# A row-streaming matmul on one core: stores moved from their own DMA ring to the ring of the loads, in a fixed order

## The chip, the core and the metric

The kernel runs on one core of a Trainium2 chip. The metric is device time in microseconds (us) of one execution, as the median of several runs. A separate profiled execution gives the trace.

## What is computed

The reference adapts a weight matrix with a low-rank product, scales each column to a given magnitude, and multiplies a long matrix of rows with it (a DoRA forward pass):

```python
batch, seq_len, in_dim, out_dim, rank = 16, 2048, 256, 256, 16
W_adapted = W + scale * (lora_A @ lora_B)
W_norm = np.sqrt(np.sum(W_adapted ** 2, axis=0, keepdims=True) + 1e-8)
W_final = W_adapted / W_norm * m
y = x.reshape(-1, in_dim) @ W_final          # (32768, 256) @ (256, 256), float32
```

The weights are small. The rows x and the result y are 33.55 MB each, and each crosses between the chip's memory (HBM) and the core's on-chip memory (SBUF) once.

## The kernel before

The 32768 rows are cut into 8 blocks (NBLK) of 4096 rows. A block is one SBUF tile `x_sb` of 128 partitions x 32 rows x 256 floats, 4 MiB. Each partition holds 32 consecutive rows, so that a transfer of a block consists of 128 pieces of 32 KB. There are five such tiles (XBUFS = 5), used in turn. The result of a block is written over the rows in the same tile, and stored from there.

At the start, small transfers bring the weights, and SP issues the loads of blocks 0 to 4 (L62, called from L77 and L78). Meanwhile the final weights `w_final` are computed (L94 to L132), once.

The main loop (L184) goes over 64 chunks (NCH), 8 (CH) per block. `transposed` casts a chunk of the rows to bf16 on GpSimd (POOL, L148), transposes it on TensorE (PE, L151), and copies the transposed chunk from PSUM to SBUF on VectorE (DVE, L155). `multiplied` does the matmuls (L166), and ScalarE (ACT, L174) copies the product over the rows in `x_sb`. In general the transposition of the next chunk is issued ahead of the product of the present one. At the last chunk of a block the product goes first.

After the last chunk of block b, ACT issues the block's store (L176). Then SP issues the load of block b+5 into the same tile (L181, which calls L62); it waits until that store has landed. The instruction order on each engine is the order of the program text. A DMA issued from SP goes to SP's ring, queue q1 in the profile; one issued from ACT to ACT's ring, queue q10. Both rings are served by the same 16 DMA engines. A transfer has landed when all of them have finished their parts.

Of the kernel before, what the change touches and what calls it, by code (L numbers as in the profile page):

```python
# [11 lines left out]
def kernel(  # L12
# [10 lines left out]
    nc = tc.nc  # L23
# [15 lines left out]
    NBLK = N // BLK  # L39
# [3 lines left out]
    XBUFS = 5  # L43
# [16 lines left out]
    def load_x(b):  # L60
        t = xpool.tile([P, DJ, IN], FP32, name="x_sb", tag="x_sb")
        nc.sync.dma_start(  # L62
            out=t,
            in_=x_flat[b * BLK : (b + 1) * BLK].rearrange("(p j) k -> p j k", p=P),
        )
        x_tiles[b] = t
# [93 lines left out]
    def multiplied(g):  # L160
        b, c = divmod(g, CH)
        xt = xts.pop(g)
        y_ps = pp_y.tile([P, J, OUT], FP32, tag="psy", name="y_ps")
        for t in range(KC):
            for j in j_order:
                nc.tensor.matmul(  # L166
                    y_ps[:, j, :],
                    xt[:, j * P : (j + 1) * P, t],
                    w_final[:, t, :],
                    start=(t == 0 and (j % (J // 2)) == 0),  # L170
                    stop=(t == KC - 1 and (j % (J // 2)) == (J // 2) - 1),
                )

        nc.scalar.copy(out=x_tiles[b][:, c * J : (c + 1) * J, :], in_=y_ps)  # L174
        if c == CH - 1:
            nc.scalar.dma_start(  # L176
                out=out_flat[b * BLK : (b + 1) * BLK].rearrange("(p j) k -> p j k", p=P),
                in_=x_tiles[b],
            )
            if b + XBUFS < NBLK:  # L180
                load_x(b + XBUFS)  # L181

    transposed(0)
    for g in range(NCH):  # L184


        first = (g + 1) % CH == 0
        if first:
            multiplied(g)
        if g + 1 < NCH:  # L190
            transposed(g + 1)
        if not first:
            multiplied(g)
# [35 lines left out]
```

## Time and profile before

| what | value |
|---|---|
| median of 5 runs | 165.04 us |
| lowest and highest of them | 164.5 and 170.71 us |
| the profiled execution's own time | 168.44 us |
| its span, first to last instruction | 166.6 us |
| mean granted TensorE clock in it | 0.873 |
| TensorE / ScalarE / GpSimd / VectorE busy | 62% / 40% / 40% / 30% |
| bytes moved by DMA, mean rate | 67.53 MB, 405 GB/s |
| from issue to landing, median of the 8 loads and of the 8 stores | 39.4 and 34.8 us |

The profiled execution is 3.4 us longer than the median of the runs: its durations are summed against 168.44 us. The page divides the span into 40 equal slices; a digit is the busy share in tenths. In DMA rows, the time from issue to landing includes the time that a transfer stands behind others on the rings. Times in the views count from the first instruction. The stores were issued at 30.81, 41.90, 52.99, 69.38, 90.07, 110.28, 130.99 and 151.46 us.

### The profile page before, as it was taken

The page shows a single profiled execution, that of the slowest core. Times are in us where ns is not written, and L with a number is a line of the kernel's source. Part 1 is how long each engine was busy: PE and PEld are TensorE (multiplying, and loading weights), DVE is VectorE, ACT ScalarE, POOL GpSimd, SP SyncE. Part 2 cuts the span into 40 slices and gives each one's busy share as a digit, 9 for nine tenths or more (in the row PEclk, how much of TensorE's full clock was granted, in tenths as well). Part 3 has the DMA queues.
Part 4 walks back from the last instruction along what each step waited for, and adds up shares of the span by engine and source line. Part 5 has one row for each costly group of instructions (what it writes and reads, how often), then busy time and mean ns, then how long its engine had stood idle before and what let it go on. Part 6 is the DMA issues. An engine that isn't in the chain of part 4 may idle for free.

```text
span 166.6 us, 2032 instructions
## 1 busy us (share of the span) xinstructions
PE 103.0 (62%) x778; PEld 86.0 (52%) x778; DVE 50.7 (30%) x76; ACT 66.4 (40%) x67; POOL 66.3 (40%) x70
## 2 busy tenths in 40 slices
PE   1174799999994699306993089920899109990000
PEld 0043588898893499204992069810698107980000
DVE  0219444444541335103350034400344003440000
ACT  3010257678576057500575007740077400773000
POOL 1007667685820972009720197101970019700000
PEclk9999999999999789975999759996599965999655
DMA  5999999999999899999999999999999999997980
GB/s 201 484 393 464 417 441 441 374 378 441 441 397 472 386 474 397 405 449 401 393 464 397 456 401 433 433 417 378 449 413 456 409 472 393 417 452 338 393 378 16
DMA packets 2635, 67.53 MB, mean 405 GB/s; under 512 B 433, under 2 KB 450, under 8 KB 578
## 3 DMA queue, kind: packets, MB, share of 16 engines
q1 hardware_dynamic: 1296, 33.82, 48.6%
q10 hardware_dynamic: 1330, 33.59, 47.1%
q8 instruction: 6, 0.10, 0.2%
q14 instruction: 3, 0.02, 0.0%
HBM read 33.85 MB, written 33.55 MB: 405 GB/s over the span
## 4 chain that ended last, share of the span: by engine, by line
DMA 53%; PE 28%; DVE 5%; ACT 2%; issue 1%; POOL 1%; ACTq 0%; POOLq 0%; SPq 0%
DMA out_dram<-x_sb 25%; DMA x_sb<-in_x_dram 25%; PE y_ps L166 18%; PE xt_ps L151 8%; DMA b_nat<-in_lora_B_dram 3%; ACT x_sb L174 2%; PE n_ps L118 1%; DVE xt L155 1%; DVE w_final L132 1%; DVE rnorm L130 1%; PE mb_ps L123 1%; POOL xb L148 1%; DVE wam L128 0%; DVE sq L113 0%; DVE wa L109 0%
## 5 line engine op out<-in xcount | busy, mean ns | idle before, releaser
L148 POOL CAST xb<-x_sb 128x1024 bf16<-128x1024 f32 x64 | 65.6, 1048 | 78.8 <-DMA x_sb<-in_x_dram 64.8
L174 ACT COPY x_sb<-y_ps 128x1024 f32<-128x1024 f32 x64 | 64.4, 1013 | 75.2 <-POOL xb L148 38.8
L166 PE MATMUL y_ps<-w_final,xt 128*128 128x256 bf16 x512 | 71.7, 289 | 1.6 <-DVE xt L155 1.6
L155 DVE COPY xt<-xt_ps 128x512 f32<-128x512 f32 x64 | 44.0, 691 | 88.1 <-PE xt_ps L151 88.1
L151 PE MATMUL xt_ps<-identity,xb 128*128 128x128 f32 x256 | 44.2, 306 | 37.7 <-POOL xb L148 37.7
L166 PEld LDWEIGHTS <-xt 128*128 128x128 bf16 x512 | 51.5, 103 | 12.0 <-DVE xt L155 4.8
L151 PEld LDWEIGHTS xt_ps<-identity,xb 128*128 128x128 f32 x256 | 34.1, 159 | 42.3 <-POOL xb L148 41.4
L120 ACT ACTIVATE norm<-n_ps,eps_col 128x256 f32<-128x256 f32 x1 | 0.5, 474 | 7.6 <-PE n_ps L118 7.6
L118 PE MATMUL n_ps<-sq,ones 128*128 128x256 f32 x4 | 2.0, 667 | 1.6 <-DVE sq L113 1.6
L98 PE MATMUL aT_ps<-identity,a_nat 128*16 128x128 f32 x2 | 0.6, 394 | 3.7 <-DMA a_nat<-in_lora_A_dram 3.7
L118 PEld LDWEIGHTS n_ps<-sq,ones 128*128 128x128 f32 x4 | 1.2, 324 | 2.2 <-issue 2.0
L104 PE MATMUL ab_ps<-b_bf,aT 16*128 16x256 bf16 x2 | 0.6, 402 | 2.8 <-DVE aT L100 2.8
L88 ACT ACT_TABLE_LOAD x1 | 1.3, 1283 | 2.2 <-issue 2.2
L98 PEld LDWEIGHTS aT_ps<-identity,a_nat 128*16 128x16 f32 x2 | 0.1, 90 | 3.7 <-issue 3.7
L94 DVE CAST b_bf<-b_nat 16x256 bf16<-16x256 f32 x1 | 0.3, 281 | 5.4 <-DMA b_nat<-in_lora_B_dram 5.4
L104 PEld LDWEIGHTS <-aT 16*128 16x128 bf16 x2 | 0.1, 104 | 3.2 <-DVE aT L100 3.2
L132 DVE TENSOR_TENSOR w_final<-wam,rnorm 128x256 bf16<-128x256 f32 x2 | 1.8, 921 | 0.0
L130 DVE RECIPROCAL rnorm<-norm 128x256 f32<-128x256 f32 x1 | 1.7, 1745 | 0.0
L125 DVE COPY m_all<-mb_ps 128x256 f32<-128x256 f32 x1 | 0.4, 425 | 3.4 <-PE mb_ps L123 3.4
L123 PE MATMUL mb_ps<-m_row,ones 1*128 1x256 f32 x2 | 1.2, 710 | 0.0
L109 DVE SCALAR_TENSOR_TENSOR wa<-ab_ps,w_nat 128x512 f32<-128x512 f32 x1 | 0.7, 691 | 0.7 <-PE ab_ps L104 0.7
L123 PEld LDWEIGHTS mb_ps<-m_row,ones 1*128 1x128 f32 x2 | 0.5, 308 | 0.7 <-issue 0.7
(12 smaller groups left out, 3.2 us busy)
## 6 DMA issues: line engine op xcount, KB each, us to landing
x_sb<-in_x_dram SPq DMA_DIRECT2D x8, 4096.0 KB, 39.4
out_dram<-x_sb ACTq DMA_DIRECT2D x8, 4096.0 KB, 34.8
w_nat<-in_W_dram SPq DMA_DIRECT2D x1, 256.0 KB, 2.7
a_nat<-in_lora_A_dram ACTq DMA_DIRECT2D x1, 16.0 KB, 2.9
b_nat<-in_lora_B_dram ACTq DMA_DIRECT2D x1, 16.0 KB, 5.2
m_row<-in_m_dram ACTq DMA_DIRECT2D x1, 1.0 KB
```

Of the source, the lines that this page charges most:

```text
L88: nc.scalar.activation(out=warm, in_=eps_col, func=AF.Sqrt)
L98: nc.tensor.transpose(aT_ps[:, t * P : (t + 1) * P], a_nat[:, t, :], identity)
L104: nc.tensor.matmul(ab_ps[:, t, :], aT[:, t * P : (t + 1) * P], b_bf, start=True, stop=True)
L118: nc.tensor.matmul(n2_ps, ones, sq[:, t, :], start=(t == 0), stop=(t == KC - 1))
L123: nc.tensor.matmul(mb_ps, ones[0:1, :], m_row, start=True, stop=True)
L130: nc.vector.reciprocal(out=rnorm, in_=norm)
L132: nc.vector.tensor_mul(out=w_final[:, t], in0=wam[:, t], in1=rnorm)
L148: nc.gpsimd.tensor_copy(out=xb, in_=rows)
L151: nc.tensor.transpose(xt_ps[:, j * P : (j + 1) * P], xb[:, j, :].bitcast(FP32), identity)
L155: nc.vector.tensor_copy(out=xt.rearrange("p r t -> p (r t)").bitcast(FP32), in_=xt_ps)
L166: nc.tensor.matmul(y_ps[:, j, :], xt[:, j * P : (j + 1) * P, t], w_final[:, t, :], start=(t == 0 and (j % (J // 2)) == 0), stop=(t == KC - ...
L174: nc.scalar.copy(out=x_tiles[b][:, c * J : (c + 1) * J, :], in_=y_ps)
```

## The change

All stores are issued by SP instead of ACT, so that loads and stores stand on one ring. The load that refills a tile is issued one block later: after store b, SP issues the load of block b+4, into the tile whose result was stored by store b-1. On SP the order becomes: loads 0 to 4, store 0, store 1, load 5, store 2, load 6, store 3, load 7, stores 4 to 7. A load still waits for the landing of the store that frees its tile, and a store for the last copy of its block.

```diff
         nc.scalar.copy(out=x_tiles[b][:, c * J : (c + 1) * J, :], in_=y_ps)
         if c == CH - 1:
-            nc.scalar.dma_start(
+            nc.sync.dma_start(
                 out=out_flat[b * BLK : (b + 1) * BLK].rearrange("(p j) k -> p j k", p=P),
                 in_=x_tiles[b],
             )
-            if b + XBUFS < NBLK:
-                load_x(b + XBUFS)
+            if b >= 1 and b - 1 + XBUFS < NBLK:
+                load_x(b - 1 + XBUFS)
```

## Prediction

> **What bounds the kernel now.** I read the busy table first, then the row of DMA shares in the 40 slices, the queue table, the chain of waits, and last the stretches of time and single transfers.
>
> ```profile
> span 166.6 us, 2032 instructions
> ...
> PE 103.0 (62%) x778; PEld 86.0 (52%) x778; DVE 50.7 (30%) x76; ACT 66.4 (40%) x67; POOL 66.3 (40%) x70
> ...
> DMA  5999999999999899999999999999999999997980
> q1 hardware_dynamic: 1296, 33.82, 48.6%
> q10 hardware_dynamic: 1330, 33.59, 47.1%
> q8 instruction: 6, 0.10, 0.2%
> ...
> x_sb<-in_x_dram SPq DMA_DIRECT2D x8, 4096.0 KB, 39.4
> out_dram<-x_sb ACTq DMA_DIRECT2D x8, 4096.0 KB, 34.8
> ```
>
> No compute engine is busy for more than 62% of the span, while the 16 DMA engines stand at nine tenths from the second slice to nearly the last. Queue q1 carries SP's ring (loads), q10 ACT's ring (stores), 33.8 and 33.6 MB. The third queue, 6 packets of instructions, will matter. In the chain, the two transfers stand for half of the span, and the long DMA pieces follow on each other:
>
> ```profile
> 52.99 42.36 DMA out_dram<-x_sb
> 95.41 41.05 DMA x_sb<-in_x_dram
> 136.60 1.05 POOL xb L148
> ```
>
> So a store issued at 52.99 takes 42 us, because it shares the engines with loads, and the load behind it another 41. A latency, however, is no loss while the engines are full. Whether they are full is in the stretches (columns: us, five engines' busy time, TensorE's clock, DMA share, GB/s):
>
> ```profile
> 3.00:30.00 27.00, 18.65 (x111) 13.89 (x112) 11.96 (x18) 8.45 (x11) 11.61 (x11) 1.00 1.00 430
> 30.00:36.00 6.00, 5.65 (x53) 5.07 (x51) 3.37 (x5) 3.85 (x5) 4.97 (x5) 1.00 0.98 358
> 36.00:53.00 17.00, 15.51 (x139) 13.58 (x137) 7.52 (x11) 13.04 (x13) 8.46 (x9) 1.00 1.01 433
> 53.00:135.00 82.00, 50.52 (x384) 42.76 (x384) 22.14 (x32) 32.20 (x32) 32.46 (x32) 0.85 1.00 424
> ...
> 150.00:154.00 4.00, 0.33 (x4) 0.05 (x1) 0.00 (x0) 1.43 (x2) 0.00 (x0) 1.00 0.81 344
> ```
>
> Loads alone on one ring run at 430 GB/s, and loads and stores alternating on two rings at 433. That is one rate, so 4 MiB cost 4.19 MB / 430 = 9.75 us, and I measure losses against it. When the first store joins (30 to 36) the rate is 358: 6 x (1 - 358/430) = 1.0 us lost. From 53 to 135, 82 x (1 - 424/430) = 1.1 us. From 150 to 154, 4 x (1 - 344/430) = 0.8 us, while the last store waits for its block. A packet is booked where it starts, so a window's edge can be off by one 32 KB packet on each of 16 engines, 0.52 MB: the 1.1 has an error of 1.2, and even the 1.0 is only good to a factor of two.
>
> The last two stores, each asked for alone:
>
> ```profile
> out_dram<-x_sb ACTq DMA_DIRECT2D x1, 4096.0 KB, 24.8
> ...
> out_dram<-x_sb ACTq DMA_DIRECT2D x1, 4096.0 KB, 14.0
> ...
> 130.99 0.34 ACTq L176 DMA_DIRECT2D out_dram<-x_sb  x1
> 151.46 0.34 ACTq L176 DMA_DIRECT2D out_dram<-x_sb  x1
> ```
>
> Store 6 lands at 131.0 + 24.8 = 155.8 and store 7 at 151.5 + 14.0 = 165.5, that is 9.7 us later: a full-rate transfer and nothing between. A landing is counted when the slowest of the 16 engines is through. So the engine that ends last had no pause before store 7. The 0.8 us at 150 to 154 were lost on engines that are ahead of it, and are worth nothing at the end. Why is one behind? The average engine needs 67.5 MB / 430 = 157 us and starts at about 3, so it could end at 160. If the 0.10 MB of instruction packets run on one engine, whose share of the rate is 430/16 = 26.9 GB/s, that one is 3.7 us later: 163.7. Add the losses of 1.0 and 1.1 and it ends at 165.8, where 165.5 is seen. That one engine fetches them all is my inference; the sum fits it.
>
> **The change, part by part.** It moves eight stores from ACT's ring to SP's, and lets the load of block b+4 follow store b (load 5 after store 1, 6 after 2, 7 after 3). No byte, packet, cast, matmul or copy is added or removed.
>
> *The issue.* ACT loses 8 issues of 0.34 us. They lie between copies of an engine that is 40% busy: worth 0. SP gets them; between its load issues it does nothing but wait.
>
> *The new order, by 9.75 us steps.* Load 0 lands at 1.2 + 12.5 = 13.7, loads 1 to 4 at 23.4, 33.2, 42.9, 52.7. Blocks are computed in about 11.1 us when loaded (stores issued at 30.8, 41.9, 53.0), so stores 0 and 1 stand on the ring when load 4 ends: 62.4 and 72.2. Load 5, issued at 62.4, lands at 81.9, then store 2 (91.7), load 6 (101.4), store 3 (111.2), load 7 (120.9), stores 4 to 7 (130.7, 140.4, 150.2, 159.9).
>
> *The added waits.* SP now waits for a block's last copy (L174) before each store, and for the store one block earlier before loads 5 to 7. Behind a waiting load stand the later stores. Load 5 waits for store 0 while store 1 still has 9.75 us on the ring; load 6 waits for store 1, 72.2, with load 5 and store 2 ahead of it, 19.5 us; load 7 for store 2, 91.7, with load 6 and store 3 ahead. What does a restart take? Before, store 0 landed at 30.8 + 24.7 = 55.5 and the load waiting for it was issued at 55.63, some 0.1 us later. The Trainium skill ("DMA: Bandwidth & Descriptors", the section on the anatomy of one DMA) gives a fixed 2.0 us per transfer, for its GpSimd path. By the row three waits would show 0.3 us, by the page about 6, if the ring were empty; since at least 9.75 us stand there, the sum takes 0 by either. The slowest engine's 3.7 us lag comes off that cover and leaves about 6.
>
> *Compute as a bound.* Block 7 lands at 120.9. In the trace, block 7's cast began at 136.60 and its store was issued at 151.46, 14.9 us. So store 7 is ready at 136 and is needed at 150: 14 us of room. Blocks 5 and 6 are ready at 97 and 116, needed at 131 and 140. TensorE's reduced clock (0.85) is in the 14.9.
>
> *Direction changes within the ring.* There are seven (load 4 to store 0, ..., load 7 to store 4), and before shows none inside one ring. From above: a cold start, load 0's 12.5 less 9.75, some 2.7 us, each: 19 us. From below: 0, or a gain, if switching once per 4 MiB is better than once per packet. The nearest row is 36 to 53, where every engine changes direction with every packet at 433 GB/s. I take 0.
>
> *What goes.* The 1.1 us from 53 to 135 and the 1.0 us at the first store lie where two rings are active and are lost on every engine, the slowest too. If the second ring causes them, 2.1 us go. From below 0: the first store's stall may belong to the first write and move to 52.7. Here a rule speaks against the change: the same page of the skill ("Issuing engines are not separate DMA queues") says that transfers issued by several engines run on the same 16 DMA engines and interleave, and that spreading them saves only issue time. By the rule the ring is indifferent and the gain is 0; by the rows it is up to 2.1. The 430 against 433 are on the rule's side, the 358 is not.
>
> **Sum.** The profiled execution took 168.44: a span of 166.6 and 1.84 around it. With all 2.1 gone the slowest engine ends at about 163.4, span 164.5, time 166.3. But the median of the runs shown is 165.04, 3.4 below that execution, and the lowest is 164.5. The ordinary runs must lack some of the profiled delays, and these stalls are the first candidates. I count two fifths of 2.1, 0.8 us, in ordinary runs: 165.04 - 0.8 = 164.2.
>
> **Rivals.**
> *No change* (about 165.0): the bytes bound, the ring makes no odds, and the slowest engine has the same packets as before. For it: 430 = 433, and 9.7 us between the last two landings. Against it: the 358.
> *All of it*: the stalls are in the ordinary runs too, 165.04 - 2.1 = 162.9. If the slowest engine also lags less there, so that the pause before store 7 reaches the end, another 0.8 goes: 162.1. Against it: the median's 3.4 us.
> *Slower, by direction changes in one ring*: if the engine finishes the last load's writes before it begins to read for the store, each change leaves a hole. At 0.4 us, 7 x 0.4 = 2.8, less the 1.1 that go with the two rings: 166.7. It decides from (1.1 + 0.5) / 7 = 0.23 us a change. For it: the stalls of before also come where transfers begin. Against it: alternation by the packet at the full rate, though there two rings supply the work.
> *The change doesn't do what it says*: if load 5 were ready only after store 1 is through, each of three loads would leave 2 us idle. The 9.75 us of cover speak against it.
>
> **How the numbers follow.** A measurement tells about 0.3%, 0.5 us, from no change. A small gain, 164.2 (163.7 to 164.7): 0.36. No change: 0.27. All of it: 0.15. Slower, including holes for unknown reasons: 0.22. Of the small gain about a fifth falls within 0.5 us and of no change a little falls on the faster side by scatter, so faster 0.46, same 0.31, slower 0.23. The range: 162.0 (all, with the pause) to 167.0 (direction changes at the price above), with more expensive ones left out.
>
> **What would show it.** Right: q10 nearly empty, q1 with 67 MB; x lands at about 43 and 53 for blocks 3 and 4 instead of 54.2 and 75.1; from 55 to 125 GB/s near 430 with no stretch of 358; SP's wait for stores moved under a full ring; the last store's issue near 136, with a landing over 25 us later. Wrong: rates under 420 between 53 and 125, holes at 52, 72, 82, 92, or the last landing at 165.5 or later in a comparable execution. If stretches are all at 430 and the time is still 165, the stalls were not in ordinary runs.

## The result and the profile after

The changed kernel takes 165.41 us (median of 44 runs, 164.86 to 166.14). Its ratio to the kernel before is 1.0017, with a 95% interval of 1.0004 to 1.003: slower by 0.17%. The interval lies above 1, but the difference is less than the 0.3% that the prediction gives as the least a measurement can tell from no change. The forecast had been 164.2, a gain of half a per cent. Left out of the ratio are long runs, more than 1.5% above a kernel's fastest, which only kernels with two rings had in number: 35 of 79 of the kernel before (median of all 79: 166.23 us, highest 173.08) and 12 of 22 of its variant below, against none of these 44 and 1 of 104 of the other one-ring runs; why is not known.

The profiled execution of the changed kernel took 165.36 us. These are its page's span, DMA shares and queues, and the landings of stores 6 and 7, counted in us from their issue:

```profile
span 163.5 us, 2035 instructions
...
DMA  5998999999999999999999999999999999999991
...
q1 hardware_dynamic: 2448, 67.37, 96.7%
q8 instruction: 6, 0.10, 0.2%
q10 hardware_dynamic: 178, 0.03, 0.1%
...
out_dram<-x_sb SPq DMA_DIRECT2D x1, 4096.0 KB, 33.3
...
out_dram<-x_sb SPq DMA_DIRECT2D x1, 4096.0 KB, 23.0
```

All large transfers are now in q1. The order on SP, from its timeline (start, us from the first to the last of the group, instruction, count):

```profile
1.16 2.90 SPq L62 DMA_DIRECT2D x_sb<-in_x_dram  x5
30.31 11.44 SPq L178 DMA_DIRECT2D out_dram<-x_sb  x2
65.50 0.34 SPq L62 DMA_DIRECT2D x_sb<-in_x_dram  x1
65.94 0.64 SPq L178 DMA_DIRECT2D out_dram<-x_sb  x1
75.18 0.34 SPq L62 DMA_DIRECT2D x_sb<-in_x_dram  x1
75.61 0.38 SPq L178 DMA_DIRECT2D out_dram<-x_sb  x1
94.55 0.34 SPq L62 DMA_DIRECT2D x_sb<-in_x_dram  x1
94.98 44.77 SPq L178 DMA_DIRECT2D out_dram<-x_sb  x4
```

Stores 6 and 7 were issued at 119.44 and 139.42, so they landed at 152.7 and 162.4: again 9.7 us apart, with nothing between. Load 5 landed at 65.50 + 19.3 = 84.8. Now the stretches of the prediction, and the one in which the first store begins (last column: GB/s):

```profile
3.00:30.00 27.00, 18.64 (x114) 13.94 (x114) 12.31 (x19) 8.94 (x11) 11.84 (x12) 1.00 1.00 429
30.00:36.00 6.00, 5.65 (x53) 5.20 (x53) 3.16 (x6) 3.85 (x5) 4.96 (x6) 1.00 1.01 429
48.00:56.00 8.00, 7.65 (x71) 6.72 (x69) 3.94 (x6) 5.85 (x6) 5.70 (x7) 1.00 1.03 389
56.00:135.00 79.00, 52.52 (x416) 45.18 (x414) 23.53 (x35) 34.42 (x36) 34.17 (x34) 0.83 1.00 431
135.00:159.00 24.00, 3.29 (x30) 2.58 (x27) 1.38 (x2) 3.80 (x4) 0.00 (x0) 0.61 1.01 433
```

The 358 of 30 to 36 us has become 429, but 389 has appeared at 48 to 56, where the ring goes from load 4 to store 0. After that the rate is 431 to the end. The stall has moved with the first store; it has not gone. In the packets of the trace it stands at the end of load 4: those that start from 50.5 to 51.1 take 1.65 to 2.03 us, and two of them 3.14 and 3.21, where 1.21 is usual.

Since a window counts whole packets at their start, I worked out the losses more finely: each packet's bytes are spread evenly over its duration, so that only what lies inside a window counts, and time lost is the window less bytes / 430 GB/s. (A steady stretch then comes out at 0 to -0.3, as its rate is 431 to 433.) In what follows "lost" means this, averaged over the 16 engines.

| execution | first large change of direction | later |
|---|---|---|
| before, the profile shown (168.44 us) | 0.90 us (30 to 38) | 1.26 us (53 to 135) |
| changed kernel (165.36 us) | 0.98 us (48 to 56) | -0.23 us (56 to 135) |

### The profile page after: what moved, and what is told of

Its sections match the earlier page's. It is cut to its first block, busy times and chain, and to the rows that moved or that the text cites. A ratio compares the mean times of both kernels' runs of the same rounds, so it can differ in the third digit from the quotient of the medians.

```text
span 163.5 us, 2035 instructions
## 1 busy us (share of the span) xinstructions
PE 99.4 (61%) x778; PEld 84.1 (51%) x778; DVE 50.5 (31%) x76; ACT 66.3 (41%) x67; POOL 66.5 (41%) x70
## 4 chain that ended last, share of the span: by engine, by line
DMA 60%; PE 16%; DVE 4%; ACT 2%; issue 1%; POOL 1%; ACTq 0%; SPq 0%; POOLq 0%
DMA out_dram<-x_sb 39%; DMA x_sb<-in_x_dram 18%; PE y_ps L166 9%; PE xt_ps L151 5%; DMA b_nat<-in_lora_B_dram 3%; ACT x_sb L174 2%; PE n_ps L118 1%; DVE w_final L132 1%; DVE rnorm L130 1%; PE mb_ps L123 1%; POOL xb L148 1%; DVE wam L128 0%; DVE wa L109 0%; DVE sq L113 0%; PE ab_ps L104 0%
## 5 line engine op out<-in xcount | busy, mean ns | idle before, releaser
L174 ACT COPY x_sb<-y_ps 128x1024 f32<-128x1024 f32 x64 | 64.3, 1012 | 63.2 <-PE y_ps L166 42.4
L166 PE MATMUL y_ps<-w_final,xt 128*128 128x256 bf16 x512 | 69.6, 283 | 2.3 <-DVE xt L155 2.3
L151 PE MATMUL xt_ps<-identity,xb 128*128 128x128 f32 x256 | 42.6, 299 | 28.5 <-POOL xb L148 28.5
L166 PEld LDWEIGHTS <-xt 128*128 128x128 bf16 x512 | 50.6, 101 | 12.2 <-DVE xt L155 5.8
L151 PEld LDWEIGHTS xt_ps<-identity,xb 128*128 128x128 f32 x256 | 33.0, 155 | 31.9 <-POOL xb L148 31.1
```

What stands on the lines that cost most here:

```text
L151: nc.tensor.transpose(xt_ps[:, j * P : (j + 1) * P], xb[:, j, :].bitcast(FP32), identity)
L166: nc.tensor.matmul(y_ps[:, j, :], xt[:, j * P : (j + 1) * P, t], w_final[:, t, :], start=(t == 0 and (j % (J // 2)) == 0), stop=(t == KC - ...
```

## The experiments

**The kernel before, profiled once more.** No edit.

> The kernel before, profiled once more, to see which of its stalls belong to an ordinary execution. Theory A (the 1.1 us between 53 and 135 us are a feature of two rings): the rate there is again near 424 GB/s against 430, and the first store's stretch (30 to 36 us) is again near 358. Theory B (the 1.1 us belong to a disturbed execution): with a span near 163.3 instead of 166.6, the rate from 53 to 135 is 428 or more, and only the first store's stall of about 1 us is left. Rival C (the span differs for another reason): span near 163.3 with both stalls as before.

It took 164.62 us, span 162.8, close to the fastest of the first five runs.

```profile
30.00:36.00 6.00, 5.65 (x53) 5.08 (x51) 2.95 (x5) 4.15 (x5) 4.29 (x5) 1.00 1.01 374
53.00:135.00 82.00, 54.00 (x398) 45.23 (x399) 23.53 (x34) 32.85 (x33) 36.36 (x37) 0.80 1.00 430
```

Theory B holds. From 53 to 135 us the two rings run at 430, not 424; the lost time there is -0.20 us. Only the first store's stall is left, 0.84 us (32 to 40). So the 1.1 us of the prediction was a property of the execution that the profile had caught, not of every execution with two rings.

**A small store at the start**, in both kernels, to see whether the first write as such is what costs.

```diff
+    touch = startup.tile([P, 32], FP32)
+    nc.vector.memset(touch, 0.0)
+    nc.scalar.dma_start(
+        out=out_flat[(NBLK - 1) * BLK : NBLK * BLK].rearrange("(p j) k -> p j k", p=P)[:, 0, 0:32],
+        in_=touch,
+    )
```

> The changed kernel with one small store (128 pieces of 128 bytes, into rows that the last store overwrites) issued from ACT at the start. Theory A (the stall at 48 to 53 us belongs to the core's first write to HBM): the stall is gone from 48 to 53, the rate there is near 430 instead of 406, all 16 engines land load 4 within about 1.5 us of each other, and the time is 1 to 3 us less than the changed kernel's 165.4. Theory B (the stall belongs to the first store on SP's ring, or to the change of direction under load): 406 again at 48 to 53, time 165.4 within 0.3. Rival C: the small store at the start holds up the weights and the first load, and the time is up to 1 us more.

165.17 us, ratio to the kernel before 1.0004 (0.9979 to 1.0028). Lost from 48 to 56: 0.91 us. The stall is there as before: theory B.

> The kernel before with the same small store from ACT at the start. Theory A (first write to HBM): the stretch from 30 to 36 us runs near 430 GB/s instead of 358 and the time falls by 1 to 3 us. Theory B (a stall of the first large store under load): 358 again, no change of time within 0.3%.

Ratio 1.0011 (0.9975 to 1.0048), and 380 GB/s from 30 to 36: the stall is there too, with 0.60 us lost from 30 to 38, somewhat smaller. Its profile has a span of 168.9 us, and from 53 to 135 it lost 1.03 us; the first profile of the kernel before (span 166.6) lost 1.26 there.

**One ring, but each load right behind its own block's store.** This undoes the second part of the change.

```diff
-            if b >= 1 and b - 1 + XBUFS < NBLK:
-                load_x(b - 1 + XBUFS)
+            if b + XBUFS < NBLK:
+                load_x(b + XBUFS)
```

> Stores on SP's ring, but each load follows its own block's store at once, as in the kernel before. SP waits for store b to land before load b+5 and before it may issue store b+1, so the ring runs empty between each store and its load, and load and next store stand behind. Theory (the later load is what keeps the single ring full): three holes of 2 to 2.7 us at load 5, 6 and 7, plus the spread of the 16 engines of about 3 us at each, so 6 to 15 us more than the kernel before, 171 to 180. Rival (the ring stays full through something else): within 0.5 us of 165.4.

178.74 us, ratio 1.0826 (1.0779 to 1.0873): as the theory said. The holes are plain (second and fourth row), and after them stands something I had not looked for (third and fifth row):

```profile
48.00:56.00 8.00, 7.65 (x70) 6.77 (x68) 3.70 (x6) 5.55 (x7) 5.92 (x6) 1.00 1.01 389
62.00:69.00 7.00, 6.65 (x61) 5.90 (x60) 3.20 (x6) 4.87 (x5) 4.98 (x6) 1.00 0.52 174
72.00:80.00 8.00, 2.24 (x20) 1.62 (x18) 0.69 (x1) 2.98 (x3) 0.37 (x1) 0.80 0.97 363
86.00:92.00 6.00, 6.00 (x57) 5.41 (x55) 3.43 (x5) 4.65 (x5) 2.08 (x2) 1.00 0.50 169
96.00:104.00 8.00, 0.36 (x2) 0.36 (x3) 0.00 (x0) 0.00 (x0) 1.45 (x2) 0.58 0.95 348
128.00:172.00 44.00, 12.51 (x96) 10.54 (x96) 5.53 (x8) 8.04 (x8) 7.05 (x7) 0.66 1.01 436
```

The first row is not a hole but the familiar stall at the first store. The holes, rows 2 and 4 and a third from 110 to 117, lost 4.2, 3.5 and 3.4 us. But where the load that follows a hole gives way to the next store (72 to 80, 96 to 104, and 120 to 128), 1.0, 1.1 and 1.1 us are lost, as at the first store. In the changed kernel the same changes from load to store cost nothing. What differs? After a hole all 16 engines start together. The landings in the trace show it: load 5's last part here comes 1.8 us after its first (77.7 to 79.5), most of them within 0.6, while in the changed kernel load 5 lands from 81.8 to 84.8. So the first store may be dear not because it is the first, but because the engines are still in step: all at the same point of their work.

**Store and load in turn from the start.** Loads 0 to 2, store 0, load 3, store 1, and so on.

```diff
-    for b in range(XBUFS):
+    for b in range(3):
         load_x(b)
...
-            if b >= 1 and b - 1 + XBUFS < NBLK:
-                load_x(b - 1 + XBUFS)
+            if b + 3 < NBLK:
+                load_x(b + 3)
```

> One ring as in the changed kernel, but store and load strictly in turn from the start: loads 0 to 2, store 0, load 3, store 1, load 4, and so on, load b+3 behind store b. Theory (the stall of about 1 us belongs to the first large store, wherever it stands, and costs the slowest engines 2 to 3 us): the stretch 48 to 53 us runs at 430 GB/s, the stall is at 30 to 36, and the time is 165.2 within 0.5. Rival (the stall of the changed kernel belongs to five loads queued ahead of the store, or to the ring's first refill): the stall stays near 48 to 53, or is gone, and the time falls by 1 to 3 us.

165.85 us, ratio 1.0054 (1.0023 to 1.0084). Neither expectation is right: at the first change (31 to 39) only 0.12 us are lost, but 0.99 at the second (39 to 47, store 0 to load 3) and 0.80 at the third (48 to 56, load 3 to store 1); afterwards nothing (-0.09 from 56 to 135).

```profile
31.00:39.00 8.00, 7.65 (x70) 6.90 (x69) 4.54 (x7) 5.51 (x6) 6.67 (x7) 1.00 1.08 457
39.00:47.00 8.00, 7.65 (x70) 6.76 (x69) 3.58 (x7) 5.59 (x6) 5.71 (x7) 1.00 0.99 375
48.00:56.00 8.00, 4.53 (x41) 3.73 (x39) 2.08 (x3) 4.74 (x5) 0.00 (x0) 1.00 0.97 373
```

The cost is not tied to the first store, nor to the direction from load to store. But the cheap first change speaks against the idea of engines in step: 15 of load 2's 16 parts had landed within 0.3 us (32.8 to 33.1). Store 0 had been issued at 31.47, only 1.3 us before its turn at about 32.8; why this change was cheap is not settled.

**Half of the matmuls.** Only the first 128 input columns are multiplied (`for t in range(1)` in the product, the stop flags to match); what is left out is the other half of the product.

> The changed kernel without the second half of the product (only the first 128 input columns are multiplied, 256 matmuls fewer), bytes unchanged. Theory A (compute is far from the bound, and instruction packets are a small part of the slowest engine's time): the instruction packets of 16 KB fall from 6 to 4 and the time from 165.4 by 0 to 0.7. Theory B (the prediction's: all instruction packets run on the one slowest engine, 0.6 us each): the time falls by 1.2 us. Rival C (compute does bound somewhere): the time falls by more than 2 us.

165.49 us, ratio 1.0018 (0.9992 to 1.0043), with four instruction packets of 16 KB instead of six:

```profile
q8 instruction: 4, 0.07, 0.2%
```

Two packets less should have freed the slowest engine of 1.2 us by the prediction's inference. Nothing came, which is theory A. TensorE is off the path, and not all instruction packets run on the engine that ends last. A second late engine does not hide a gain: the last three parts of store 7 land at 161.8, 162.5 and 162.6, in the changed kernel at 161.5, 162.3 and 162.4.

**Nine tiny loads behind the last store**, to see which engines end last.

```diff
+    for n, k in enumerate((15, 14, 12, 8, 7, 6, 4, 2, 1)):
+        probe = startup.tile([P, 32], FP32, name=f"probe{n}")
+        nc.sync.dma_start(out=probe[0:k, :], in_=x_flat[0:k, 0:32])
```

> The changed kernel with nine tiny loads (15, 14, 12, 8, 7, 6, 4, 2 and 1 partitions of 128 bytes) on SP's ring behind the last store. A load of k partitions lands in k parts, on k of the engines; each part stands behind the last store's packets on its engine, so the landings tell how far behind each group of engines is. Theory A: one and the same one or two engines are 3 us behind from the first store on, and they show in some of the groups and not in others. Theory B: the spread is shared over many engines: all groups show it alike. The time is that of the changed kernel plus 1 to 3 us.

One execution, 166.88 us. The parts of three of these loads landed at (us, from the trace's semaphore updates; each load is some 0.2 us later than the one before):

```
7 partitions: 160.2 160.9 160.9 161.1 162.8 163.4 163.5
6 partitions: 160.4 161.0 161.1 161.3 163.0 163.6
4 partitions: 160.6 161.2 161.3 161.5
```

The Trainium skill ("DMA: Bandwidth & Descriptors", the section on why a DMA increments its semaphore by 16) says that such a transfer of k partitions runs on the k lowest-numbered engines. The lists are nested as that wants. Going from 7 to 6 loses the latest part, from 6 to 4 the two that were then latest: counted from 0, engine 6, and engines 4 and 5, are the late ones, 1.7 us or more behind the other four. It is theory A with three engines. In the changed kernel the spread is there before 56 us: load 3's parts land from 42.4 to 42.8, but for one at 44.2; load 4's from 52.6 to 53.2, but for two at 55.7; store 7's from 159.2 to 162.4. So one engine is late before the stall, two are 2.5 us late after it, and 3.1 of the final spread of 3.2 us are there when it ends. (The landings carry no engine numbers, so that these are the same engines is likely, not shown.)

**Engines out of step from the start.** To test the idea of engines in step: extra loads on few engines, ahead of the others, of rows that are loaded again afterwards. These loads alone add bytes. (`load_x` then takes the tiles made here; that part of the edit is not shown.)

```diff
+    for b in range(XBUFS):
+        first_tiles[b] = xpool.tile([P, DJ, IN], FP32, name="x_sb", tag="x_sb")
+    for b, k in ((2, 12), (3, 8), (4, 4)):
+        nc.sync.dma_start(out=first_tiles[b][0:k], in_=x_flat[b * BLK : (b + 1) * BLK].rearrange("(p j) k -> p j k", p=P)[0:k])
     for b in range(XBUFS):
         load_x(b)
```

> The changed kernel with three extra loads at the start, of 12, 8 and 4 partitions of 32 KB (rows that are loaded again afterwards). They run on the first 12, 8 and 4 DMA engines, so that the engines reach the first store in four groups, 1.2 us apart, instead of together. 24 extra packets of 1.21 us on 16 engines are 1.8 us on the average and 3.6 us on the first four. Theory A (the stall comes from all engines changing from loads to stores at the same moment): the loss of 1.0 us on the average, 406 GB/s at 48 to 53, is spread out or gone; from 48 to 62 us the mean rate is 425 or more, and the time is 0.5 to 2 us above the changed kernel's, not 3. Theory B (the stall belongs to the first large store as such): the loss stays at about 1 us on each group, and the time is 2 to 4 us above.

176.98 us, ratio 1.0722 (1.0681 to 1.0763): the time misses both expectations, for a reason of its own. The extra loads and those behind them ran at 136 GB/s from 3 to 18 us. But from there on the kernel is at full rate, and the stall is gone: the first store now begins as load 4's parts land, from 63.3 to 67.1.

```profile
58.00:74.00 16.00, 15.65 (x143) 14.19 (x142) 7.92 (x12) 11.85 (x12) 12.12 (x13) 1.00 1.00 425
74.00:135.00 61.00, 38.07 (x300) 32.25 (x298) 16.80 (x25) 26.36 (x27) 22.12 (x22) 0.84 1.00 432
```

Lost from 58 to 74: 0.09 us.

**The same without extra bytes**: the load of block 1 in parts of 112, 12 and 4 partitions.

```diff
+        rows = x_flat[b * BLK : (b + 1) * BLK].rearrange("(p j) k -> p j k", p=P)
+        for lo, hi in ((0, 112), (112, 124), (124, 128)) if b == 1 else ((0, P),):
+            nc.sync.dma_start(out=t[lo:hi], in_=rows[lo:hi])
```

> The changed kernel with the load of block 1 in three parts of 112, 12 and 4 partitions, on 16, 12 and 4 engines: engines 0 to 3 carry one packet more (1.21 us), engines 12 to 15 one less. The last landings of the tiny loads put engines 4 to 6 last, 2.5 to 3 us behind the first, and 0 to 3 in the first half. Theory A (moving together is what stalls): the stall is smaller for the slowest engines and the time falls by 0.5 to 1.5 us, below both kernels. Theory B (the first store as such): the slowest engines carry what they carried, time as the changed kernel's within 0.3 us.

178.32 us, ratio 1.0809 (1.0769 to 1.0848): neither theory's time. It was to be the version that beats both kernels, and the split load spoiled it:

```profile
12.00:39.00 27.00, 14.86 (x98) 11.68 (x96) 10.47 (x14) 8.05 (x8) 8.47 (x8) 0.90 0.99 195
58.00:74.00 16.00, 15.65 (x143) 14.19 (x142) 7.87 (x13) 11.75 (x13) 12.12 (x12) 1.00 1.01 430
```

27 us at under half of the rate lost 14 us. Again the engines arrive out of step (load 4's parts land from 65.2 to 68.4), and the first store, which follows, costs next to nothing: 0.05 us lost from 58 to 74.

**Out of step, with every fourth partition.** The same extra loads, but of partitions 0, 4, 8 and so on, so that each of the few engines serves its own group of partitions.

```diff
-    for b, k in ((2, 12), (3, 8), (4, 4)):
+    for b, k in ((4, 4), (3, 4)):      # the other kernel: ((4, 8),)
-        ...[0:k]
+        ...[0 : 4 * k : 4]
```

> The changed kernel with two extra loads at the start, each of the 4 partitions 0, 4, 8, 12 (32 KB each, loaded again afterwards): two packets more, 2.4 us, on the first four DMA engines alone, which had 2.2 us or more to spare at the end. Theory A (the stall is 16 engines changing direction together, and every fourth partition keeps one engine to one group of partitions): the loads run at 430 GB/s from 8 us on; engines 0 to 3 reach the first store 2.4 us behind the others; the stall from 48 to 56 us falls from 1.0 to 0.7 or less; time within 1 us of 165.4. It beats both kernels only if the three last engines are spared. Theory B (the stall is that of a first store, the skew only hid it): still 1.0, and time 165.4 to 167.

> As before, but one extra load of the 8 partitions 0, 4, ..., 28: one packet more, 1.2 us, on the first eight engines. Two groups of eight, 1.2 us apart, instead of sixteen together. Theory A: the stall from 48 to 58 us is half of 1.0 or less, and the time is that of the changed kernel plus 1.2 us (three of the last engines are among the eight) less what they are spared of the stall, 164.5 to 166. Theory B: the stall stays at 1.0, time 166.5 or more.

The loads now run near full rate from 8 to 30 us: at 427 GB/s with eight engines delayed, and with four:

```profile
8.00:30.00 22.00, 13.36 (x86) 10.52 (x85) 8.45 (x13) 5.66 (x7) 10.07 (x10) 1.00 1.00 430
```

For the stall, whole packets are too coarse (405 to 408 GB/s from 48 to 62 in both and in the changed kernel). By bytes within the window:

| kernel | intended at the first store | parts of load 3 land | lost from 48 to 62 us |
|---|---|---|---|
| changed kernel | all together | over 1.8 us (15 within 0.4) | 1.05 us |
| one packet more on 8 engines | two groups of 8 | over 2.2 us | 0.61 us |
| two packets more on 4 engines | 4 behind 12 | over 2.7 us (11 within 0.4) | 0.36 us |
| load 1 in parts (58 to 74 us) | not in groups | over 3.2 us | 0.05 us |
| 12, 8 and 4 partitions (58 to 74 us) | four groups | over 3.8 us | 0.09 us |

From 1.05 us down to under 0.1, the loss is smaller where the engines are further apart. That is in favour of theory A, and the first store as such is excluded. But it is a trend in five kernels, each with other side effects, and two changes in the alternating kernel do not fit: the cheap first one, and the fourth (store 1 to load 4), which cost nothing (-0.02 us from 59 to 67) although 13 of load 3's 16 parts had landed within 0.4 us and all within 2.3. So spread is not the whole condition.

The expectations are met only in part. With four engines delayed the stall is in the range, but the time is 166.49 (ratio 1.0102, 1.0078 to 1.0126), 1.1 above the changed kernel instead of within 1; with eight, 0.61 us is more than the half expected, and the time of 167.14 (1.0105, 1.004 to 1.0169) is theory B's. The slow start of the extra loads, 321 and 357 GB/s from 3 to 8 us, costs more than the stall gives back. No version here beats the two kernels.

## Why the prediction was wrong

*What it had right.* The bound: with half of the matmuls the time stayed where it was. The order on the ring and its cover: from 56 us on the ring is never empty, and one_ring_old_order shows what happens without the later load, 13 us more. The waits of SP cost nothing. Compute has room: store 7 was issued at 139.4 for a turn at about 150 (forecast: 136). The pause before store 7 was worth nothing: the second profile of the kernel before has none (store 7 was issued at 145.82, store 6 landed at 152.0), and 9.7 us between the last two landings stayed. Changes of direction inside the ring were put at 0: right from the second on, while the first cost 0.98 us.

*The step that failed is "what goes".* It took 1.0 + 1.1 us for losses to the second ring and booked two fifths of them, 0.8 us, as a gain in ordinary runs. Neither term came; the change made the kernel 0.28 us slower.
- The 1.1 us from 53 to 135: -0.20 us in the second profile of the same kernel. The working had said that the 1.1 has an error of 1.2, and that the ordinary runs must lack some of the delays; it should have drawn the conclusion that a term of the size of its error, in an execution 3.4 us too long, is no gain.
- The 1.0 us at the first store: 0.98 in the changed kernel, 18 us later. The prediction's lower bound, that the stall moves to 52.7, is what happened.

So the rival "no change", 165.0, was the case. The rule of the skill that spoke against the change, that transfers of several issuing engines interleave on the same 16 DMA engines and spreading them saves only issue time, agrees with the runs: 430 GB/s on two rings (53 to 135 us, second profile) and 431 on one (56 to 135).

*The inference about instruction packets* fell too. With four packets instead of six nothing changed, so they do not all run on the engine that ends last; and three engines are late, mostly since the stall. The sum of 165.8 against 165.5 had fitted by luck: the 3.7 us of packets stood for delays from elsewhere.

*The rival that direction changes leave holes* had a piece of the truth: a change of direction can cost about 1 us on the average engine, 0.8 to 1.1 in six places of the two kernels one_ring_old_order and alternate. But in the changed kernel only the first does; the later ones are free (-0.23 us from 56 to 135), probably because the engines are by then apart. So it is paid about once, by either kernel.

*What stays open.* Why the changed kernel is 0.28 us (0.17%) slower. In the one profile of each, the last part of store 7 lands 3.2 us after the first in the changed kernel (159.2 to 162.4) and 2.3 in the kernel before (159.4 to 161.7). Whether the stall treats the late engines worse behind five loads, one profile of each cannot tell. Nor is it shown what it is that engines in step contend for, what makes a change free besides spread, or why engines 4 to 6 lose most.

Moving the loads alone, with the stores left on ACT, was not run: SP would issue the same loads in the same order with the same waits as before.

## What to carry to other kernels

Where the transfer engines are at their full rate, count gains from a new transfer order only against stalls seen in an execution as long as the median; profile again when the profiled time is off by more than the gain. One ring was as fast as two, to 0.2%, so long as something always stood behind a waiting transfer: here the later load is what makes the single ring possible, and without it 8% are lost. When a stall sits at a place in the program, ask what it belongs to before booking it as removed: the place, the resource, or the state in which all engines arrive.

## What the runs showed of the hardware

- A change of direction that the sixteen engines reach nearly together cost 0.8 to 1.1 us on the average, but in the alternating kernel one cost 0.12 us and one nothing; with the engines spread over 3 us it cost under 0.1. An empty ring brings them back into step: load 6 of one_ring_old_order, issued after a hole, lands in parts from 101.9 to 102.4.
- A transfer to a part of the partitions can slow all that stands behind it: 195 GB/s with 112, 12 and 4 neighbouring partitions, 136 with 12, 8 and 4. With every fourth partition the following loads were at 430. This fits the port map in the Trainium skill ("SBUF — State Buffer", the section on the DMA port swizzle), where four neighbouring partitions share one of 16 ports, so that several engines would share one; the runs show the rates, not the ports.
